# Query and key heads stored unrotated, forget gates in steps, and a second phase in written TensorE order

## The chip, the cores and the metric

The kernel runs on one core of one Trainium2 chip. The metric is the device time of one execution in microseconds. Before the change it is 2653.64 us, the median of 3 runs (2651.35 to 2655.81).

## The reference

The reference is a trunk of two layers over 1024 positions of width 1024, float32. Layer 0 mixes with gated DeltaNet heads and a short convolution (`mixer_ab`), layer 1 with HGRN2 heads and dilated sliding-window attention (`mixer_cd`). Each layer adds a SwiGLU feed-forward network of 2816 hidden columns, and a normalisation closes the trunk. The change lies in `mixer_cd`, cut here to what matters:

```python
hq, hf, hi, hg, sq, sk, sv = split_cols(h @ w_in, CD_SPLITS)      # 4 x 512 and 3 x 1536 columns
f_gate = lb + (1 - lb) * sigmoid(hf);  log_f = log(f_gate);  k_in = (1 - lb) * sigmoid(-hf)
o_c = hgrn2_recurrence(silu(hq), k_in, hi, log_f)                 # 4 heads, 128 x 128 state, chunks
o_c = rms_norm(o_c, norm_g) * sigmoid(hg)
sq, sk = rope(sq, pos), rope(sk, pos)                             # 3 patterns x 4 heads of 128
for p, (window, dilation) in enumerate(((128, 1), (512, 4), (2048, 16))):
    o_p, lse_p = dilated_window_attention(sq[p], sk[p], sv[p], window, dilation)
o_d = sum over p of softmax(lse)[p] * o_p
return concatenate([o_c, o_d]) @ w_out

def rope(x, pos):                                                 # x1, x2: halves of the 128 columns
    return concatenate([x1 * cos - x2 * sin, x1 * sin + x2 * cos])
```

## The kernel before

Activations stand transposed, features on the 128 partitions and positions along the free dimension, in two halves of 512 positions. Weights and activations are split into a high and a low float32r part, and each product of a 128x128 block runs as three matmuls (`mm3`, lines 126 to 128). `split` (lines 102 and 103) makes the two parts: a ScalarE cast for the high one and a VectorE subtraction for the low one.

**The pair loop.** The class `Up` (line 253) computes two column blocks of a projection at a time, as one product of 2x2 blocks: the halves of the positions by the halves of the inner dimension, with seven products instead of eight (`p1`, `p2`, `p5`, `p6`, `p7` and the two at the end of a pair). A product is 12 matmuls of 512 columns. GpSimd makes the sums of weight blocks (`sums`, `sums_late`, lines 302 to 308), `part_a` to `part_d` split them. In both feed-forward networks `Up.pair` runs in this way for 22 pairs. `Pairs` (line 726) is a subclass that does it for 16 pairs of layer 1's input projection: 12 pairs of a query and a key head (`"k"`, pattern, head), and 4 of an HGRN2 forget gate and query (`"f"`, head). Its loop starts at line 898. Everything in it, on TensorE, VectorE, ScalarE, GpSimd and the DMA queue of SyncE, stands in an order written out by hand (`manual_schedule`): an engine takes its instructions in the order of the source, and what stands behind a waiting one waits too.

A finished block c of a rotated head goes through `roped` (line 775): ScalarE copies the two halves of the partitions crosswise (L778, L779), GpSimd multiplies the copy by the sines (L780), VectorE multiplies c by the cosines (L781) and adds (L785, or L789 with a strided store which puts the positions of a dilated pattern in order of their residue classes). The result goes to DRAM (`qk`). `forget` (line 794) makes the gates of one block in four parts. These are generators; the loop advances them with `next` at chosen places. The copies and sums that TensorE waits for stand between them: `snap` (L338), the copy of x in `p6` (L365), the copy and sum in `add22` (L825, L826), `add11` (L342), and `row1`'s sum (L838).

Raw weights come through two buffers of a ring and a spare one; those for the next pair are asked for at the end of a pair and at the start of the next.

**The second phase.** `mixer_cd` (line 1659) projects the values with plain `mm3` products: `hgrn_v` for HGRN2 (two calls of eight row blocks), `swa_v` for a pattern of attention, `hgrn_gates` for the output gates. After each piece they call `tick(cost)`, which advances two generators in turn, `chain` (the units of HGRN2, a head and a half each) and `local` (the attention). A turn of `local` computes the scores of one quarter of an attention head, the transposes of the quarter before, and the outputs of the one before that; a head is four turns. `Attend` loads q and k of a head from DRAM, `combine` merges the three patterns. `rate` sets how many turns a unit of cost gives.

In this phase no order is written: a planner puts the instructions of each engine in order by the place in the source and by the time at which it expects them to be ready, and draws instructions forward whose inputs and buffers are there.

A unit of HGRN2 (line 1710) computes decays for seven block sizes on VectorE and ScalarE (`decayed`, L1722 to L1730), products of 32x32 blocks (`blocks`, L1738), the update of the state (L1819), outputs (L1823, L1826), their norm (L1829 to L1838) and a product with a diagonal (L1844), in seven pieces of TensorE work.

Of the kernel before, what the change touches and what calls it, by code (L numbers as in the profile page):

```python
# [54 lines left out]
def hybrid_trunk_kernel(ctx: ExitStack, tc: tile.TileContext, x_t, w_all, w_down, w_ba, vecs, c_f, c_i, c_rope, out):  # L55
# [670 lines left out]
    class Pairs(Up):  # L726

        early = True
        HEADS = (("k", 0, 0), ("k", 0, 1), ("k", 0, 2), ("k", 0, 3), ("k", 1, 0), ("f", 0), ("k", 1, 1), ("k", 1, 2),
                 ("f", 1), ("k", 1, 3), ("k", 2, 0), ("f", 2), ("k", 2, 1), ("k", 2, 2), ("f", 3), ("k", 2, 3))  # L730

        def __init__(self, left):
# [7 lines left out]
            self.snaps = self.right = None  # L740

        def src(self, kind, f):
# [20 lines left out]
        def turned(self):  # L763
            return self.right.tile([P, HT], F32, tag="r", name="r", bufs=2)

        def done(self, f, i, half, c, psum=False):

            kind = self.HEADS[f]
            if kind[0] == "k":
                return self.roped(self.qk[kind[1:]][i, :, half], kind[1], half, c, psum)  # L770
            if i == 0:
                return self.forget(self.bkq[kind[1], half], kind[1], c)
            return self.query(self.bkq[kind[1], half], c, psum)

        def roped(self, dst, p, half, c, psum):
            t = slice(half * HT, (half + 1) * HT)
            r = self.turned()
            S.copy(r[0:64], c[64:128])  # L778
            S.copy(r[64:128], c[0:64])  # L779
            G.tensor_tensor(r, r, self.rope[:, 1, t], op=MULT)  # L780
            V.tensor_tensor(c, c, self.rope[:, 0, t], op=MULT)  # L781
            yield
            if p == 0:
                d = r if psum else c
                V.tensor_tensor(d, c, r, op=ADD)  # L785
            else:
                n = (None, 4, 16)[p]
                d = self.scratch("d")
                V.tensor_tensor(d.rearrange("p (r i) -> p i r", r=n), c.rearrange("p (i r) -> p i r", r=n),  # L789
                                r.rearrange("p (i r) -> p i r", r=n), op=ADD)  # L790
            dma(dst, d)
            yield

        def forget(self, dst, h, c):
            r = self.turned()
            V.tensor_scalar(c, c, -44.0, None, op0=MAX)
            S.activation(r, c, AF.Exp, scale=-1.0)
            S.activation(c, r, AF.Identity, bias=onec[:, 0:1])
            yield
            V.reciprocal(c, c)  # L800
            d = self.scratch("d")
            G.tensor_tensor(d, r, c, op=MULT)
            yield
            S.activation(r, c, AF.Ln, scale=self.omlb[:, h:h + 1], bias=self.lb[:, h:h + 1])
            S.activation(d, d, AF.Copy, scale=self.omlb[:, h:h + 1])
            dma(dst[1], d)
            yield
            for j in range(4):
                t = slice(j * P, (j + 1) * P)
                V.tensor_tensor_scan(c[:, t], onec[:, 0:1].to_broadcast([P, P]), r[:, t], 0.0, op0=MULT, op1=ADD)  # L810
            dma(dst[0], c)
            yield

        def query(self, dst, c, psum):
            r = self.turned()
            S.activation(r, c, AF.Tanh, scale=0.5)
            yield
# [80 lines left out]
        def pair(self, f, count, b11, b21, b22, t1, t2, t3, t4):  # L898
# [31 lines left out]
            if more:  # L930
                s = self.sums(an, bn)
# [1445 lines left out]
```

## Time and profile before

| what | us |
|---|---|
| median of 3 runs | 2653.64 |
| the profiled execution | 2653.08 |
| its span, from the first to the last instruction | 2651.3 |
| pair loop of layer 1, pairs 3 to 14 | 285.6 (1216.4 to 1502.0) |
| last pair | 30.2 (1502.0 to 1532.2) |
| second phase, up to the output projection | 381.9 (1532.2 to 1914.1) |

Layer 0 and its feed-forward network lie ahead of these stretches, the output projection and the feed-forward network of layer 1 behind them. The page's busy time of TensorE is 97% of the span; since matmuls are pipelined and their ends are modelled, the number of matmuls in a stretch says more about it than the busy time.

### The profile page before, as it was taken

To read this page: it belongs to the slowest core of one execution; us is meant where nothing else is said; L and a number is where in the kernel's file an instruction comes from. 1 tells how busy PE (TensorE), PEld (TensorE's weight loads), DVE (VectorE), ACT (ScalarE), POOL (GpSimd) and SP (SyncE) were. 2 spreads that over 40 slices of the span, in tenths; PEclk is the share of its full clock that TensorE was granted. 3 is DMA by queue.
4 is the path that set the end of the run, shared out by engine and by line. 5 is a ranking of instruction groups with operands and counts; after the bars stand their busy time and mean duration, and the time that the engine had idled before them with its cause. 6 is when DMAs were issued, how large, how long until landed. Compare 5 with 4: busy or idle time off the path is not lost. (4 is left out here: it accounts for less than half of the span.)

```text
span 2651.3 us, 37844 instructions
## 1 busy us (share of the span) xinstructions
PE 2571.7 (97%) x14163; PEld 2131.2 (80%) x14163; DVE 1750.8 (66%) x2873; ACT 1076.2 (41%) x1779; POOL 656.1 (25%) x552
## 2 busy tenths in 40 slices
PE   8999999999999999998888899999999999999998
PEld 6888888888888888887666687978788888888887
DVE  7887775685655665578777776358867655556554
ACT  5432123343333344445545544445444333334442
POOL 1110111333333200135545411000023433331001
PEclk9999999999999999999999999999999999999999
DMA  4425447325566687623323344666672555658853
GB/s 140 139 94 167 110 144 237 117 95 179 175 210 204 223 288 265 195 80 111 100 96 104 111 160 128 168 157 199 178 237 71 168 171 184 216 200 290 279 176 119
DMA packets 273480, 443.12 MB, mean 167 GB/s; under 512 B 48624, under 2 KB 133136, under 8 KB 273040
## 3 DMA queue, kind: packets, MB, share of 16 engines
q1 hardware_dynamic: 273296, 440.71, 51.3%
q8 instruction: 111, 1.82, 0.3%
q14 instruction: 73, 0.60, 0.1%
HBM read 300.55 MB, written 140.07 MB: 166 GB/s over the span
## 5 line engine op out<-in xcount | busy, mean ns | idle before, releaser
L103 DVE TENSOR_TENSOR w<-raw,w 128x1024 fp32r<-128x1024 f32 (+1 forms) x323 | 387.4, 1204 | 142.3 <-ACT w L102 141.0
L102 ACT CAST w<-raw 128x1024 fp32r<-128x1024 f32 (+1 forms) x323 | 307.9, 958 | 284.8 <-PE psu L128 152.2
L126 PE MATMUL psu<-hnh,w 128*128 128x512 f32 x848 | 338.4, 399 | 7.6 <-ACT w L102 7.6
L127 PE MATMUL psu<-hnl,w 128*128 128x512 f32 x848 | 332.0, 392 | 0.1
L128 PE MATMUL psu<-hnh,w 128*128 128x512 f32 x848 | 332.0, 391 | 0.0
L126 PEld LDWEIGHTS psu<-hnh,w 128*128 128x128 f32 x848 | 160.2, 189 | 40.1 <-ACT w L102 7.6
L128 PEld LDWEIGHTS psu<-hnh,w 128*128 128x128 f32 x848 | 159.8, 188 | 34.6 <-DVE w L103 0.8
L127 PEld LDWEIGHTS psu<-hnl,w 128*128 128x128 f32 x848 | 160.3, 189 | 32.7 <-DVE hnl L2162 0.7
L187 POOL TENSOR_TENSOR acc<-acc,sq 128x512 f32<-128x512 f32 x48 | 70.5, 1469 | 430.2 <-ACT sq L183 410.7
L302 POOL TENSOR_TENSOR ws<-raw 128x512 f32<-128x512 f32 x54 | 75.7, 1403 | 399.0 <-DMA raw<-in_dram 255.4
L103 DVE TENSOR_TENSOR w<-ws,w 128x1024 fp32r<-128x1024 f32 x51 | 73.2, 1436 | 97.7 <-ACT w L102 97.7
L103 DVE TENSOR_TENSOR hidq<-hr,hidq 128x1024 fp32r<-128x1024 f32 x72 | 82.4, 1145 | 77.3 <-ACT hidq L102 77.1
L126 PE MATMUL psu<-t3h,w 128*128 128x512 f32 x240 | 98.7, 411 | 24.6 <-ACT u L365 24.4
L102 ACT CAST hidq<-hr 128x1024 fp32r<-128x1024 f32 x72 | 70.2, 979 | 103.7 <-DMA hr<-ts 62.3
L126 PE MATMUL psm<-hidq,w 128*128 128x512 f32 (+1 forms) x275 | 106.0, 385 | 0.0
L127 PE MATMUL psm<-hidq,w 128*128 128x512 f32 (+1 forms) x275 | 105.8, 385 | 0.0
L128 PE MATMUL psm<-hidq,w 128*128 128x512 f32 (+1 forms) x275 | 105.8, 385 | 0.0
L780 POOL TENSOR_TENSOR r<-r,rope 128x512 f32<-128x512 f32 x48 | 80.6, 1682 | 97.9 <-ACT r L779 90.9
L126 PE MATMUL psu<-t4h,w 128*128 128x512 f32 x240 | 95.0, 396 | 9.0 <-ACT c L825 8.5
L126 PE MATMUL psg<-b22h,w 128*128 128x512 f32 x216 | 85.8, 397 | 12.6 <-DVE c L826 12.6
L127 PE MATMUL psu<-t3l,w 128*128 128x512 f32 x240 | 96.7, 403 | 0.0
L128 PE MATMUL psu<-t3h,w 128*128 128x512 f32 x240 | 96.7, 403 | 0.0
(507 smaller groups left out, 6775.2 us busy)
## 6 DMA issues: line engine op xcount, KB each, us to landing
raw<-in_dram SPq DMA_DIRECT2D x227, 512.0 KB, 4.0
sd<-in_dram SPq DMA_DIRECT2D x44, 512.0 KB, 3.9
hid<-hid SPq DMA_DIRECT2D x88, 256.0 KB, 2.8
sd<-sd SPq DMA_DIRECT2D x44, 512.0 KB, 3.4
hr<-ts SPq DMA_DIRECT2D x40, 512.0 KB, 4.6
raw<-sd SPq DMA_DIRECT2D x40, 512.0 KB, 4.4
hd<-h SPq DMA_DIRECT2D x48, 256.0 KB, 3.8
h<-hd SPq DMA_DIRECT2D x48, 256.0 KB, 5.8
```

Of the source, the lines that this page charges most:

```text
L102: S.copy(hi, src)
L103: eng.tensor_tensor(lo, src, hi.bitcast(F32), op=SUB)
L126: T.matmul(o, lh, rh, start=first and i == 0, stop=False, **kw)
L127: T.matmul(o, lh, rl, start=False, stop=False, **kw)
L128: T.matmul(o, ll, rh, start=False, stop=last and i == n - 1, **kw)
L187: (eng or G).tensor_tensor(a, a, q, op=ADD)
L302: G.tensor_tensor(s[:, HT:], b[:, :HT], b[:, HT:], op=ADD)
L780: G.tensor_tensor(r, r, self.rope[:, 1, t], op=MULT)
```

## The change

A head's q and k are stored as they come out of the projection, in the order of the residue classes. The rotation moves to the second phase: `Attend` loads q and k, and loads each once more with the two halves of the partitions exchanged (`rs`, four DMAs), and GpSimd multiplies the exchanged copy by the sines (`sines`) and q or k by the cosines, and adds (`roped`): twelve operations of 128x512 a head. There are three tables of cosines and sines, one for each order of positions. The work of a head's rotation is spread over the turns of the head before.

The gates are computed for both halves together, in seven steps, of which a pair takes three (`step`). The order of the 16 pairs changes. Raw weights are asked for a pair earlier, for even pairs into the spare buffer and a new one, for odd pairs into the ring.

The second phase has TensorE in written order. A unit of HGRN2 has its block products in two runs, and outputs in a third; its norm is taken from sums that ScalarE makes beside the square, and it scales before four transposes, which take the place of the product with a diagonal. HGRN2's values go through DRAM. The second `hgrn_v` stands ahead of the second pattern. `combine` scales and adds with the weight as a scalar operand, 128 columns at a time.

```diff
-        HEADS = (("k", 0, 0), ("k", 0, 1), ("k", 0, 2), ("k", 0, 3), ("k", 1, 0), ("f", 0), ("k", 1, 1), ("k", 1, 2),
-                 ("f", 1), ("k", 1, 3), ("k", 2, 0), ("f", 2), ("k", 2, 1), ("k", 2, 2), ("f", 3), ("k", 2, 3))
+        HEADS = (("k", 0, 0), ("k", 0, 1), ("k", 0, 2), ("f", 0), ("k", 1, 0), ("k", 1, 1), ("f", 1), ("k", 1, 2),
+                 ("k", 1, 3), ("f", 2), ("k", 2, 0), ("k", 2, 1), ("f", 3), ("k", 2, 2), ("k", 2, 3), ("k", 0, 3))
...
+        def fetch(self, n):
+            if n >= len(self.HEADS):
+                return
+            if n % 2:
+                self.coming[n] = self.raw("g", n), self.raw("u", n)
+                return
+            t = self.right.tile([P, DM], F32, tag="raw", name="raw", bufs=1)
+            self.coming[n] = self.raw("g", n, True), t
+            dma(t, self.src("u", n))
...
-            r = self.turned()
-            S.copy(r[0:64], c[64:128])
-            S.copy(r[64:128], c[0:64])
-            G.tensor_tensor(r, r, self.rope[:, 1, t], op=MULT)
-            V.tensor_tensor(c, c, self.rope[:, 0, t], op=MULT)
...
+        def total(self, f, i, half, c, y):
+            if (self.HEADS[f][0], i) == ("f", 1):
+                V.tensor_tensor(c, c, y, op=ADD)
+                return self.query(f, half, c)
+            d = self.place(f, c)
+            o, a, b = self.streams(f, d, c, y)
+            V.tensor_tensor(o, a, b, op=ADD)
+            self.keep(f, i, half, d)
...
+        def forget(self, h):
+            cs = [self.kept_f.pop((h, half)) for half in range(NH)]
+            rs = [self.scratch("fr") for _ in cs]
+            for c, r in zip(cs, rs):
+                V.tensor_scalar(c, c, -44.0, None, op0=MAX)
+                S.activation(r, c, AF.Exp, scale=-1.0)
             yield
+            for c, r in zip(cs, rs):
+                S.activation(c, r, AF.Identity, bias=onec[:, 0:1])
             yield
+            for half, (c, r) in enumerate(zip(cs, rs)):
+                V.reciprocal(c, c)
+                d = self.fresh("kk")
+                V.scalar_tensor_tensor(d, r, self.omlb[:, h:h + 1], c, op0=MULT, op1=MULT)
+                dma(self.bkq[h, half][1], d)
+                yield
+            for c, r in zip(cs, rs):
+                S.activation(r, c, AF.Ln, scale=self.omlb[:, h:h + 1], bias=self.lb[:, h:h + 1])
             yield
...
+        def pair(self, f, b11, b21, b22, t1, t2, t3, t4):
             n = f + 1
             self.p1(f, b11)
+            if f == 3:
+                self.fetch(n)
             self.add22(f - 1)
...
+                self.part_d(f, self.a)
+                self.fetch(n + 1)
+            self.step()
             self.p2(f, b21, psm())
             g = self.snap(f)
...
             self.add11(f, g)
+            an, bn = self.coming.pop(n)
+            s = self.sums(an, bn)
+            self.row2(f - 1, t4)
+            self.part_a(n, an)
+            self.sums_late(an, bn, s)
+            self.row1(f - 1, b22)
+            self.step()
             self.p6(f, t2)
             self.p5(f, t1, psg())
+            self.part_b(n, s)
+            self.part_c(n, bn)
+            self.a = an
+            self.step()
+            self.p7(f, t3)
...
                 def __init__(self, h, p):
+                    if p not in table:
+                        table.clear()
+                        table[p] = tl("rope", (2, 2, HT))
+                        dma(table[p], c_rope[p].rearrange("p z (b t) -> p z b t", b=2))
+                    self.table, self.w = table[p], []
+                    for src in (pairs.qk[p, h][i] for i in range(2)):
+                        w = tl("rs", (2, HT), 2)
+                        dma(w[0:64], src[64:128])
+                        dma(w[64:128], src[0:64])
+                        self.w.append(w)
...
+                def sines(self, i):
+                    for b in range(2):
+                        G.tensor_tensor(self.w[i][:, b], self.w[i][:, b], self.table[:, 1, b], op=MULT)
+                def roped(self, i):
...
+                    for b in range(2):
+                        G.tensor_tensor(c[:, b], c[:, b], t[:, b], op=MULT)
+                        G.tensor_tensor(c[:, b], c[:, b], w[:, b], op=ADD)
...
+                for p in range(3):
+                    for j in range(4):
+                        d, x, w = t[0][:, j, 0:P], t[p][:, j, 0:P], w3[:, p, j:j + 1]
+                        if p:
+                            V.scalar_tensor_tensor(d, x, w, d, op0=MULT, op1=ADD)
+                        else:
+                            S.activation(d, x, AF.Copy, scale=w)
...
+                def begin():
+                    u = first.pop()
+                    second.append(u)
+                    u.load()
+                    todo[:] = [lambda: [u.sines(i) for i in (1, 0)], lambda: u.roped(1), lambda: u.roped(0), prepare]
...
+                    if not now and second:
+                        while todo:
+                            todo.pop(0)()
+                        now += [second.pop(), 0]
+                        if first:
+                            begin()
+                    elif todo:
+                        todo.pop(0)()
...
-            due, rate = [0.0, 0.0], [0.0, 4 / 3]
+            due, rate = [0.0, 0.0], [0.0, 1.0]
...
+            with tc.manual_schedule(engines={E.PE}):
+                hgrn_v(0, pairs.first, lambda cost: None, range(0, 4))
+                have_v[0] = 1
+                hgrn_v(0, pairs.first, tick, range(4, 8))
+                for p in (1, 2, 0):
+                    swa_v(p, tick)
+                    ready += [(h, p) for h in range(4)]
+                    rate[0] = 1.4 if p == 0 else 0.8
+                    if p == 1:
+                        hgrn_v(1, wload(("cd", 10), ("cd", 11)), tick)
+                        have_v[0] = 2
+                hgrn_gates(tick)
+                while ready or busy[0]:
+                    next(loc)
```

More of the change, by code (lines that the diff above doesn't have):

```diff
@@ L1798, in hgrn @@
[L1798 to L1808 removed]
+                last = half == NH - 1
@@ L1809, in hgrn @@
+                for r in range(4):
+                    z = slice(r * 32, (r + 1) * 32)
+                    S.copy(attn[z, :, z], ac[z])
                 before = [states.get(h)] + [st[:, c, :] for c in range(3)]
@@ L2111, in local @@
                     line = [line[1], nxt]
-                    busy[0] = any(line) or bool(late or now or ahead or ready)
+                    busy[0] = any(line) or bool(late or now or second or first or ready)
                     yield
@@ L2131, in mixer_cd @@
                 G.memset(diag[i], 0.0)
[L2132 to L2144 removed]
+            E = mybir.EngineType
+            with tc.manual_schedule(engines={E.PE}):
[12 more added lines that the diff above has]
+                    next(loc)
     es = ExitStack()
```

512 lines of the change are left out of this document (220 added, 292 removed).

## The prediction

> **What bounds the kernel now.** I read the page first. TensorE is busy 97% of the span, but the page says that a busy PE is not a PE at its peak, so the next view was the table of busy time by stretches, cut at the first matmuls of the stages. Its columns are: stretch, length, then busy us and count of PE, weight loads, DVE, ACT and POOL, granted clock, DMA share, GB/s.
>
> ```profile
> span 2651.3 us, 37844 instructions
> PE 2571.7 (97%) x14163; PEld 2131.2 (80%) x14163; DVE 1750.8 (66%) x2873; ACT 1076.2 (41%) x1779; POOL 656.1 (25%) x552
> ...
> 1138.90:1216.40 77.50, 73.39 (x322) 60.20 (x321) 71.20 (x76) 37.58 (x50) 31.76 (x18) 0.96 0.28 92
> 1216.40:1502.00 285.60, 246.34 (x1009) 194.70 (x1008) 210.32 (x209) 147.32 (x207) 152.49 (x94) 0.95 0.29 96
> 1502.00:1532.20 30.20, 25.65 (x109) 19.95 (x108) 24.26 (x26) 20.38 (x27) 12.09 (x8) 1.00 0.41 132
> 1532.20:1655.00 122.80, 119.48 (x1424) 100.42 (x1424) 80.54 (x202) 51.91 (x103) 16.16 (x24) 1.00 0.47 155
> 1655.00:1740.00 85.00, 85.00 (x642) 76.19 (x640) 32.01 (x118) 39.57 (x115) 3.44 (x6) 1.00 0.63 160
> 1740.00:1806.70 66.70, 64.24 (x809) 51.97 (x805) 47.05 (x170) 36.26 (x106) 6.70 (x12) 1.00 0.59 163
> 1806.70:1914.10 107.40, 100.84 (x985) 85.85 (x983) 92.00 (x328) 54.54 (x148) 6.67 (x11) 0.98 0.63 185
> 2100.00:2400.00 300.00, 300.00 (x1326) 248.39 (x1325) 179.13 (x237) 101.88 (x142) 105.56 (x80) 1.00 0.59 196
> ```
>
> The last row is the yardstick: the feed-forward loop of layer 1 issues 1326 matmuls in 300.0 us, 0.2262 us each, with no gap. The pair loop of the CD projection (second row of stretches) has the same products and issues 12 pairs x 84 = 1008 of them; at 0.2262 that is 228.0 us, and it takes 285.6. So 57.6 us of TensorE are lost there, and 30.2 - 108 x 0.2262 = 5.8 in the last pair. The reader is to see that this loop, and not the kernel as a whole, has a second limit. The view of waits for that loop names it:
>
> ```profile
> POOL r L780 <- ACT r L779: 71.3, 23, 8.0
> ACT r L778 <- DVE c L826: 36.6, 8, 6.0
> PE psu L126 <- ACT u L365: 24.4, 11, 4.9
> DVE d L789 <- POOL r L780: 20.5, 11, 4.6
> PE psg L126 <- DVE c L826: 12.6, 10, 2.9
> PE psu L126 <- ACT c L825: 6.7, 6, 1.5
> ```
>
> PE waits for plain copies out of PSUM (L365, L825) and the add behind one (L826): 43.7 us. They are late because the rotation, ACT L778/L779 to POOL L780 to DVE L789, stands in the same queues in written order. In the phase behind it, 1532.2 to 1914.1 (381.9 us), the waits of PE are few:
>
> ```profile
> PE psu L2067 <- DVE ol L2062: 4.8, 2, 3.2
> PE psg L1844 <- DVE e L1838: 2.4, 3, 1.0
> PE psg L1738 <- issue: 2.3, 2, 1.5
> PE psg L1793 <- DVE m L1730: 0.7, 1, 0.7
> ```
>
> **Part 1, the pair loop: about -60.** Out go, per rotated head, eight ACT half copies, four POOL products, four DVE products by the cosine and the adds; in come only the sums of the products (strided for two patterns).
>
> ```profile
> L103 DVE TENSOR_TENSOR w<-ws,w 128x1024 fp32r<-128x1024 f32 x13 | 22.5, 1734 | 0.0
> L789 DVE TENSOR_TENSOR d<-psu,r 128x512 f32<-128x512 f32 x7 | 7.6, 1088 | 0.0
> L342 DVE TENSOR_TENSOR gt<-gt,psm 128x512 f32<-128x512 f32 x13 | 8.8, 676 | 0.0
> L800 DVE RECIPROCAL gt<-gt 128x512 f32<-128x512 f32 x4 | 13.4, 3342 | 0.0
> L338 ACT COPY gt<-psu 128x512 f32<-128x512 f32 x13 | 7.6, 581 | 0.2
> L804 ACT ACT_TABLE_LOAD x8 | 10.3, 1283 | 0.1
> L780 POOL TENSOR_TENSOR r<-r,rope 128x512 f32<-128x512 f32 x43 | 73.6, 1714 | 74.0 <-ACT r L779 71.3 <-DVE w L103 2.5
> L308 POOL TENSOR_TENSOR raw<-raw,ws 128x512 f32<-128x512 f32 x13 | 23.5, 1811 | 0.0
> ```
>
> DVE then has, per rotated pair, three strided sums at 1.09, three weight remainders at up to 1.73 and half a one: about 9 us of the pair's 228.0/12 = 19.0. The feed-forward loop hides 179.1/300 = 60% of DVE, 11.3 us a pair, without a gap, so TensorE should set the pace; what is late next is the strided sums, which only stores and a free PSUM bank wait for. A forget gate adds, over the three pairs in which its seven steps run, two reciprocals (6.7), small work of about 5 and a few table loads at 1.28; its longest piece, 3.34, is shorter than the 5.4 us (24 matmuls) between a product's end and the next one that needs its copy. The gates cost 0 if those 5.4 us hold, and 8 x 3.34 = 26.7 if every reciprocal lands ahead of a wait; I take 4, near the first, since the feed-forward row shows none. The strided copy on ACT in row2 isn't in the trace: between 0.58 (L338) and the DVE ratio 1088/676 of it, 0.93; nothing waits for it but a DMA. Fetching raw weights a pair ahead issues the same DMAs earlier on SP's queue, behind stores that wait for DVE; with 19 us of lead I cost that at nothing, and at 4 us a pair if the lead is gone. Loop: 57.6 - 4 = -53.6. Last pair: 5.8 less the one copy and one add that still stand between p7 and the last two products (0.58 + 0.68, so 1.2): -4.6. The opening (first stretch: 322 x 0.2262 = 72.8 of 77.5) can give 0 to 4; I take 2. Sum: -60.2.
>
> **Part 2, the second phase: about +5.** Rows of that phase, then the queues of DVE and POOL at one place of the loop before:
>
> ```profile
> L1844 PE MATMUL psg<-e,e 128*128 128x128 f32 x64 | 8.9, 281 | 2.5 <-DVE e L1838 2.4
> L1800 PE MATMUL psg<-cf,kk 128*128 128x128 f32 x32 | 5.1, 280 | 0.0
> L1838 DVE TENSOR_TENSOR e<-cf,rr 128x512 f32<-128x512 f32 x8 | 5.5, 693 | 8.7 <-POOL rr L1836 8.7
> L1833 DVE TENSOR_REDUCE ss<-e 128x4 f32<-128x512 f32 x8 | 5.5, 685 | 3.4 <-ACT e L1831 3.3
> L1846 DVE TENSOR_SCALAR e<-psg,vec 128x512 f32<-128x512 f32 x8 | 6.0, 748 | 2.7 <-PE psg L1844 2.6
> k<-qk SPq DMA_DIRECT2D x12, 512.0 KB, 4.8
> ```
> ```profile
> 1359.97 2.32 DVE L103 TENSOR_TENSOR w<-ws,w 128x1024 fp32r<-128x1024 f32 x1
> ...
> 1365.13 1.23 DVE L103 TENSOR_TENSOR w<-raw,w 128x1024 fp32r<-128x1024 f32 x1 [1.13 <-ACT w L102]
> ...
> 1359.91 1.30 POOL L307 TENSOR_TENSOR raw<-raw 128x512 f32<-128x512 f32 x1
> 1361.17 2.28 POOL L308 TENSOR_TENSOR raw<-raw,ws 128x512 f32<-128x512 f32 x1
> ```
>
> HGRN2's last product becomes four transposes a half: 8.9 to 5.1, -3.8. Three longer runs, two turns apart, should remove the waits at L1844, L1793 and L1738: 3 to 5 of the rows above, I take 4. DVE loses the reduction, the diagonal and the scaling by the gain (5.5 + 5.5 + 6.0 = 17 us in all), which is off the path.
>
> Against that stand the rotations: 12 attention heads x 12 GpSimd products or sums of 128x512. One alone is 1.30 (L307). The queues show what it does to DVE: the remainder issued at 1359.97, under L307, took 2.32 for 1.23, that is, it began its work when L307 ended at 1361.21; and L308, issued at 1361.17, took 2.28, waiting out that remainder. So a POOL operation and a DVE operation with two SBUF operands exclude each other. Per POOL operation DVE loses between 0 and 2.32 - 1.23 = 1.1; the phase-long means lie between (w<-ws 1.73 in the loop against 1.23 free: 0.5), and I take 0.55: 144 x 0.55 = 79 us. DVE has 381.9 - (80.5 + 32.0 + 47.1 + 92.0) = 130 idle, so on the whole it fits, but not in the last stretch, where 15.4 are idle and three heads (36 operations, 20 us) fall: about 5 over. A rotation takes 12 x 1.30 = 15.6 free, 12 x 1.71 = 20.6 at the mean of L780, 27.4 if each is blocked as L308 was; the last stretch gives 22.4 attention turns (16 ticks at 1.4) in 107.4 us, 4.8 a turn, 19.2 a head. At 20.6 the scores, which in written order hold all of TensorE behind them, come 1.4 late per head, 5 in four heads. I take 10 for both. The written order leaves 54.4 turns inside the projections where 55 are needed (three turns stay empty while the second pattern's values aren't there): the last combination stands bare, +3. The partner halves, three sine tables and the value round trip add some 20 MB to a DMA share of 0.47 to 0.63; I cost it at nothing, because q and k are asked for early, and at 4.8 (the k row) per load if not. SP issues some 75 DMAs more at 0.33 (L1922, quoted below), 25 us of a queue that is mostly empty; but a partner load that waits for its tile to be released by POOL holds the weights and stores behind it on SP, and this is where a late rotation would spread. Phase: -3.8 - 4 + 10 + 3 = +5, ends -12 and +35.
>
> The Trainium skill, "SBUF — State Buffer", section "Who interferes with whom", says that VectorE and GpSimd share one port pair as an exclusive lock, and that whichever starts second is fully blocked; the two rows above agree. By it the sum stays as it is, but it speaks against this change: rival A is its full price.
>
> **Sum.** The profiled execution took 2653.1 us (span 2651.3 and 1.8 around it), the median of the runs is 2653.6: no difference to speak of. 2653.1 - 60.2 + 5 = 2598.
>
> **Rivals.** A, the shared port decides the second phase: each POOL operation holds DVE 0.95 instead of 0.55 (137 us). DVE's own work is 251.6 - 17 - 5 = 230; its busiest stretch reached 92.0/107.4 = 0.857, and (230 + 137)/0.857 = 428 is 46 more than 381.9. Then 2653.1 - 60.2 + 46 = 2639. For it: the rows of L103 and L308, and that decays come in rows of short two-operand operations. Against: POOL is idle in the first stretch and can work ahead there. It decides from 0.68 us an operation on.
>
> B, slower than before: no head start. The first head of each pattern is loaded, rotated and scored in one turn of the written order. If its loads and products aren't drawn forward, TensorE stands for table and operands (4.8) and 12 x 1.71: 25.3, three times, 76: 2653.1 - 60.2 - 7.8 + 76 = 2661. It decides from 68/3 = 22.7 us a start on. Against it: before, the first q load was issued at 1545.6 and its scores began at 1625.9, 80 us later, so loads are drawn forward.
>
> ```profile
> L1950 PE MATMUL psm<-k,q x128: 270/379/631, 1625.9 to 1893.1; 128*128 128x256 f32 x88, 128*128 128x128 f32 x40
> L1922 SPq DMA_DIRECT2D q<-qk x8: 319/330/1066, 1545.6 to 1846.4; - x8
> ```
>
> C, the pair loop keeps half of its loss, because the forget steps put reciprocals and table loads ahead of the copies: +27 (the bound above), 2625. D, the second phase gains too (-18: all waits of the four rows, the transposes, and rotations wholly under idle DVE): 2575.
>
> **Numbers.** Forecast 0.60 (2598, own range 2580 to 2618), A 0.14, B 0.04, C 0.11, D 0.11. The range 2568 to 2638 holds the forecast, C, D and the nearer half of A. A measurement here tells 0.2% (5.3 us) from no change; faster holds in all cases but B and the upper tail of A: 0.94; same 0.02; slower 0.04.
>
> **What would show it.** Right: the twelve pairs take 229 to 238 us with 1008 matmuls; no wait of PE for L365's copy; POOL busy some 200 to 250 us in the second phase, two-operand DVE groups there with means above their present ones, PE's waits gathered in the last stretch at the scores. Wrong: pairs still above 21 us (part 1), or a second phase over 400 us (A), or three PE waits over 20 us at the first scores of a pattern (B).

## The result, and the profile after

The changed kernel takes 2675.64 us, the median of 4 runs (2671.94 to 2678.84), against 2652.49 us (2650.50 to 2655.81) of the kernel before in the same comparison: a ratio of 1.0089 with a 95% interval of 1.0076 to 1.0101. It is slower by 23 us, where 2598 us and "faster" were forecast. The profiled execution took 2674.45 us, 21.4 us more than the 2653.08 us of before.

The table of busy time by stretches of the kernel after, cut at the same stages as before; columns as in the prediction. The last stretch but one runs from the end of the pairs to the first matmul of the feed-forward network's norm, so it holds the second phase and the output projection:

```profile
1138.90:1212.10 73.20, 70.34 (x322) 57.83 (x322) 63.69 (x70) 33.46 (x44) 25.91 (x14) 1.00 0.31 109
1212.10:1440.55 228.45, 228.45 (x1010) 189.22 (x1008) 144.47 (x142) 99.68 (x133) 75.29 (x50) 1.00 0.32 115
1440.55:1466.00 25.45, 25.45 (x115) 21.05 (x114) 13.39 (x20) 11.26 (x15) 1.03 (x3) 1.00 0.62 212
1466.00:1989.10 523.10, 444.57 (x4048) 376.83 (x4048) 344.15 (x838) 230.70 (x631) 214.34 (x158) 0.92 0.63 185
2120.00:2420.00 300.00, 300.00 (x1325) 248.43 (x1324) 177.81 (x238) 101.62 (x142) 104.15 (x80) 1.00 0.58 195
```

The same view of the kernel before, for the stretch from the end of its pairs to the same norm:

```profile
1532.20:1967.80 435.60, 423.26 (x4085) 358.71 (x4085) 281.71 (x849) 204.38 (x501) 41.88 (x59) 1.00 0.61 181
```

The pair loop did what was forecast: 12 pairs in 228.45 us instead of 285.6, with 1.00 of the clock and no idle time, the yardstick's pace. With the opening (73.20 for 77.50) and the last pair (25.45 for 30.20) it gives 66.2 us. All of that and 21.3 more is lost behind it: 523.10 for 435.60 is +87.5. TensorE stands idle there for 523.10 - 444.57 = 78.5 us instead of 12.3, and its busy time grew by 21.3 with no more matmuls. The granted clock fell from 1.00 to 0.92. The clock record of this stretch knows full and half clock only; 14 pieces of it, of 3.4 to 10.2 us and 85 us together, are at half clock.

The waits of TensorE in that stretch, after (engine, tile and line, what ended the wait: us in all, times, longest):

```profile
PE psg L1834 <- ACT e L1758: 20.2, 7, 5.5
PE psu L2088 <- DVE ol L2081: 20.0, 10, 6.3
PE psm L1968 <- DVE stat L1974: 13.9, 3, 5.5
PE psm L2026 <- DVE pt L2017: 6.6, 2, 4.5
```

Transposes (L1834), the combination (L2088), scores (L1968) and outputs (L2026) all wait a little, for VectorE or for ScalarE's copy L1758; for a rotated operand of GpSimd they wait 0.3 us in all. What happens to VectorE shows in its own groups. Line, engine, operation, names and shapes, count, then busy us and mean ns, after:

```profile
L1719 DVE TENSOR_TENSOR m<-m,q 128x256 f32<-128x256 f32 x56 | 39.7, 709 | 1.6 <-DMA q<-bkq 1.5
L1711 DVE TENSOR_TENSOR m<-b 128x256 f32<-128x256 f32 x56 | 37.6, 676 | 26.7 <-PE psg L1727 23.9 <-DMA kk<-bkq 2.7
L1715 DVE TENSOR_TENSOR m<-m,kk 128x256 f32<-128x256 f32 x48 | 34.7, 724 | 1.9 <-ACT m L1714 1.7
L1713 DVE TENSOR_TENSOR m<-b 128x256 f32<-128x256 f32 x48 | 30.6, 638 | 0.0
L1974 DVE CUSTOM_DVE_ANT_0 sc<-psm,cf 128x256 f32<-128x256 f32 x44 | 17.7, 419 | 7.0 <-PE psm L1968 7.0
```

The same four groups of the decays in the kernel before:

```profile
L1730 DVE TENSOR_TENSOR m<-m,q 128x256 f32<-128x256 f32 x56 | 23.7, 423 | 1.5 <-ACT m L1728 1.5
L1722 DVE TENSOR_TENSOR m<-b 128x256 f32<-128x256 f32 x56 | 23.6, 427 | 14.6 <-PE psg L1738 14.0 <-PE psg L1793 0.3
L1726 DVE TENSOR_TENSOR m<-m,kk 128x256 f32<-128x256 f32 x48 | 20.3, 424 | 6.0 <-ACT m L1725 5.6
L1724 DVE TENSOR_TENSOR m<-b 128x256 f32<-128x256 f32 x48 | 20.4, 425 | 0.0
```

In this kernel the tiles `psm`, `psg` and `psu`, which TensorE writes, lie in PSUM, and VectorE's other operands in SBUF. The four groups, each with two operands in SBUF, take 638 to 724 ns in the mean, where they took 423 to 427. The group of L1974 has one operand in PSUM and takes the same 419 ns (416 before).

Two places of the timeline after, with start, us, engine, line and count, show how this reaches TensorE (a row that is three operations in one says x3 and the time from its first to its last):

```profile
1840.06 1.19 DVE L2071 TENSOR_TENSOR tmp<-w,cm 128x4 f32<-128x4 f32 x1
1841.28 1.18 DVE L2073 TENSOR_TENSOR dn<-dn,tmp 128x4 f32<-128x4 f32 x1
...
1857.24 0.17 DVE L2071 TENSOR_TENSOR tmp<-w,cm 128x4 f32<-128x4 f32 x1
1857.44 0.16 DVE L2073 TENSOR_TENSOR dn<-dn,tmp 128x4 f32<-128x4 f32 x1
1857.64 0.18 DVE L2074 RECIPROCAL tmp<-dn 128x4 f32<-128x4 f32 x1
1857.85 2.23 DVE L2076 TENSOR_TENSOR w<-w,tmp 128x4 f32<-128x4 f32 x3
1860.00 3.75 DVE L2081 SCALAR_TENSOR_TENSOR ol<-cm,w,ol 128x128 f32<-128x128 f32 x6
...
1841.18 2.48 POOL L1944 TENSOR_TENSOR q<-q,rope 128x512 f32<-128x512 f32 x2
1857.57 4.98 POOL L1937 TENSOR_TENSOR rs<-rs,rope 128x512 f32<-128x512 f32 x4 [11.46 <-DMA rs<-qk]
...
1856.44 1.06 PE L2026 MATMUL psm<-vp,pt 128*128 128x128 f32 x8
1863.01 0.48 PE L2088 MATMUL psu<-cf,ol 128*128 128x128 f32 x1 [5.51 <-DVE ol L2081]
...
1865.88 0.63 PE L126 MATMUL psu<-hnh,w 128*128 128x512 f32 x1
1866.31 0.63 PE L127 MATMUL psu<-hnl,w 128*128 128x512 f32 x1
```

`combine` divides four numbers a row by their sum. While GpSimd is idle, one such step takes 0.16 us (L2073 at 1857.44). Beside GpSimd's products it takes 1.18 (1841.28): an operation on 4 columns costs as much as one of GpSimd's on 512. At 1857.57 GpSimd starts four products of a head's rotation, three steps take 2.23 us and the sums behind them 3.75 for six. TensorE waits 5.51 us for the end of that chain. In the kernel without rotations (below) such a step takes 157 ns and such a sum 347 in the mean; by these, an estimate, 3.4 of the 5.51 us come from GpSimd. Then TensorE's matmuls of 512 columns start 0.43 us apart (1865.88, 1866.31), where 0.2262 is its pace at full clock, and the stretch around it was granted half the clock:

```profile
1862.00:1868.50 6.50, 5.18 (x14) 3.86 (x15) 2.44 (x8) 0.59 (x1) 0.55 (x1) 0.50 0.61 149
```

The clock fell inside the wait, some 4.4 us after the last matmul and before the next one:

```profile
1860.00:1861.00 1.00, 0.00 (x0) 0.00 (x0) 1.00 (x2) 0.69 (x2) 1.00 (x2) 1.00 0.00 0
1862.00:1863.00 1.00, 0.00 (x0) 0.00 (x0) 1.00 (x3) 0.00 (x0) 0.55 (x1) 0.50 0.00 0
```

The same is to be found all over the stretch: TensorE has 12 waits of 2.9 us or more in it, and at each of them, within 4 us of its end, a piece at half clock begins. In the kernel before, the one wait of that size in its stretch (3.2 us) has such a piece too.

The Trainium skill, "TensorE: Matmul & The Clock Gate", section "Part 1: The HAM clock gate", says that the array falls to half its clock after an idle window of about 3.4 us; the trace agrees, with the wait of 5.51 us and these rows. Two of the 12 waits, of 2.95 and 3.05 us, are shorter than that window and have a piece at half clock all the same.

### The profile page after: what moved, and what is told of

Read it like the earlier page. It is cut to its first block, busy times and chain, and to the rows that moved or that the text cites. A ratio compares the mean times of both kernels' runs of the same rounds, so it can differ in the third digit from the quotient of the medians.

```text
span 2672.6 us, 37762 instructions
## 1 busy us (share of the span) xinstructions
PE 2572.3 (96%) x14131; PEld 2143.1 (80%) x14131; DVE 1727.8 (65%) x2786; ACT 1041.8 (39%) x1815; POOL 733.3 (27%) x600
## 5 line engine op out<-in xcount | busy, mean ns | idle before, releaser
L302 POOL TENSOR_TENSOR ws<-raw 128x512 f32<-128x512 f32 x54 | 81.8, 1514 | 428.5 <-DMA raw<-in_dram 299.6
L103 DVE TENSOR_TENSOR w<-ws,w 128x1024 fp32r<-128x1024 f32 x51 | 66.6, 1306 | 113.8 <-ACT w L102 113.8
L308 POOL TENSOR_TENSOR raw<-raw,ws 128x512 f32<-128x512 f32 x51 | 67.0, 1314 | 161.1 <-DVE w L103 161.1
L393 POOL TENSOR_TENSOR hid<-hid,c 128x512 f32<-128x512 f32 x44 | 62.3, 1416 | 126.0 <-ACT hid L392 125.8
L126 PE MATMUL psu<-t4h,w 128*128 128x512 f32 x240 | 93.7, 391 | 0.5 <-ACT c L372 0.5
L127 PE MATMUL psu<-t4l,w 128*128 128x512 f32 x240 | 93.4, 389 | 0.0
L128 PE MATMUL psu<-t4h,w 128*128 128x512 f32 x240 | 93.4, 389 | 0.0
L126 PE MATMUL psu<-t3h,w 128*128 128x512 f32 x240 | 93.4, 389 | 0.0
```

Source lines behind the costliest of these rows:

```text
L103: eng.tensor_tensor(lo, src, hi.bitcast(F32), op=SUB)
L126: T.matmul(o, lh, rh, start=first and i == 0, stop=False, **kw)
L127: T.matmul(o, lh, rl, start=False, stop=False, **kw)
L128: T.matmul(o, ll, rh, start=False, stop=last and i == n - 1, **kw)
L302: G.tensor_tensor(s[:, HT:], b[:, :HT], b[:, HT:], op=ADD)
L308: G.tensor_tensor(a[:, HT:], a[:, HT:], s[:, :HT], op=SUB)
```

## The experiments

Each kernel below is the changed one with the edit shown. The theory from the trace: a GpSimd product or sum of two SBUF operands keeps VectorE's two-operand operations waiting, these stand in chains that TensorE waits for, and the written TensorE order lets it do nothing else meanwhile.

### The rotation, and the written order

Without the rotation (`sines` and `roped` return at once; q and k are used unrotated, and all loads stay):

```diff
 def sines(self, i):
+    return
 def roped(self, i):
+    return
```

> The changed kernel without the twelve GpSimd operations of a head: q and k are used unrotated, so the attention is that of unrotated heads; all loads stay. Theory 2: VectorE's busy time in the second phase falls from 315 to about 235 us, the phase to about 390 and the kernel to 2580 to 2600. Theory 1: the phase falls by less than 30 us and the kernel stays above 2645. Theory 3: the waits at L1834 stay at 20 us.

Measured: 2597.86 us (2594.49 to 2602.05), ratio 0.9796 (0.9781 to 0.9810). The 144 operations cost 2675.64 - 2597.86 = 78 us, not 10, as the second theory had it. Its stretch from the end of the pairs to the norm, and its group for L1719:

```profile
1466.00:1908.80 442.80, 419.48 (x4049) 359.46 (x4048) 250.53 (x838) 228.36 (x631) 17.13 (x14) 0.98 0.74 218
```
```profile
L1719 DVE TENSOR_TENSOR m<-m,q 128x256 f32<-128x256 f32 x56 | 23.5, 419 | 1.8 <-DMA q<-bkq 1.7
```

VectorE does the same 838 operations in 250.53 instead of 344.15 us: 93.6 us, or 0.65 for each of the 144 operations on GpSimd.

The second phase in the planner's order:

```diff
-with tc.manual_schedule(engines={E.PE}):
+with ExitStack():
```

> The changed kernel with its second phase in the planner's TensorE order again; all else as changed. Theory 1 (the written order costs it: TensorE stands at the head of its line where other products were ready): the second phase falls from 470 us by 60 or more, the kernel to 2590 to 2615. Theory 2 (GpSimd's rotations hold VectorE through the shared port, and the order only shows it): VectorE's busy time in the phase stays near 315 us and the kernel stays above 2645. Theory 3 (a third PSUM bank in one turn, 20 us of waits at L1834): about 2655.

Measured: 2655.94 us (2653.38 to 2662.96), ratio 1.0020 (1.0010 to 1.0029). 20 us of the loss hang on the order in which TensorE takes its work. The first theory, by which the order made the whole loss, is out.

Both edits together:

> Both at once: no rotation (unrotated q and k are used) and the planner's TensorE order. It gives the floor of the phase: 355 to 370 us, the kernel 2555 to 2575. If theories 1 and 2 are two sides of one thing (late VectorE work that only a written order makes TensorE stand for), it is no more than 15 us under the better of the two single runs; if they are two costs that add, it is lower than each by what the other gave.

Measured: 2584.57 us (2578.88 to 2590.24), ratio 0.9745 (0.9728 to 0.9762), above the floor of 2555 to 2575 that was expected. Without rotations the written order costs 13 us, fewer than the 20 beside GpSimd. The waits show where most of it lies; first without rotations in written order, then in the planner's:

```profile
PE psg L1834 <- ACT e L1758: 12.9, 7, 2.5
```
```profile
PE psg L1834 <- ACT e L1758: 3.5, 5, 1.5
```

L1834 are the transposes that close the HGRN2 unit before. One of these waits in the timeline of the changed kernel:

```profile
1529.34 1.30 ACT L1714 ACTIVATE m<-m 128x512 f32<-128x512 f32 x2 [1.90 <-DVE m L1713]
1530.55 0.57 ACT L1758 COPY e<-psg 128x512 f32<-128x512 f32 x1
...
1531.17 1.11 PE L1834 MATMUL psg<-cf,e 128*128 128x128 f32 x4 [2.95 <-ACT e L1758]
```

They start when ScalarE's copy L1758 has emptied a PSUM buffer, which stands in ScalarE's queue behind exponentials that wait for VectorE's decays. In written order TensorE stands at them until then.

Those transposes one turn later:

```diff
-                ending[1]()
                 ms = [decayed(8, *bkq), decayed(16, *bkq)]
                 yield
+                ending[1]()
```

> The changed kernel with the four transposes that close a unit of HGRN2 one turn later, so that they don't ask for a third bank of a tag that has two in the turn that fills both. Theory 3: the waits of TensorE at L1834 (20.2 us in seven places) go, and the kernel falls by 15 to 25 us, to about 2655. Theories 1 and 2: they move to the next place where VectorE or ScalarE is late, and the kernel moves by less than 8 us.

Measured: 2667.78 us, ratio 1.0064 (1.0047 to 1.0081): 8 us less; the main loss stays. But the 8 us don't come from where the third theory looked for them: TensorE's waits at L1834 stay at 17.0 us in seven places, after 20.2, and those of the scores (L1968) fall from 13.9 to 6.4. So the theory of the third bank is out.

### What of the rotation costs

Three things could cost: rotated operands that come late, a long queue on GpSimd (the power of HGRN2's norm, L1825, stands in it), or the port through which GpSimd and VectorE both read SBUF, the prediction's shared port. The first kernel runs twelve such operations a head on the exchanged copies and tables alone, whose results nobody reads (q and k are used unrotated):

```diff
-    c, w, t = self.c[i], self.w[i], self.table[:, 0]
-    if len(c.shape) == 4:
-        w, t = (x.rearrange("p b (s i) -> p b s i", s=16) for x in (w, t))
+    c, w, t = self.w[i], self.w[i], self.table[:, 0]
...
-        G.tensor_tensor(c[:, b], c[:, b], w[:, b], op=ADD)
+        G.tensor_tensor(c[:, b], c[:, b], t[:, b], op=ADD)
```

> The changed kernel with the same twelve GpSimd operations a head, at the same places, but all of them on the exchanged copies and the tables: q and k are used unrotated, and no score waits for GpSimd. What it tells apart: the rotated operands come late (then it falls to where no rotation stood, 2590 to 2615), or the operations cost by running beside VectorE, whoever needs their results (then VectorE's busy time in the second phase stays near 315 us and the kernel at 2660 to 2680). I expect the second.

Measured: 2692.45 us (2684.49 to 2695.89), ratio 1.0145 (1.0125 to 1.0165). No score waits for a rotation here, and it is slower still. But it isn't a clean test: VectorE waits 63.9 us for the power in it, and 20.4 in the changed kernel, since all twelve operations of a head stand in the queue at once. So it was run again with the power left out (`V.tensor_scalar(rr, ss, 1.0, None, op0=ADD)` in its place):

> The twelve operations of the decoy, whose results nobody reads, and the power left out as well (the heads aren't normalised, q and k not rotated), so that no engine waits for a result of GpSimd. Theory (the read port alone makes the cost): 2650 to 2685, at least 50 us above the 2598 us without operations on GpSimd. Rival (the decoy's cost came from the power standing behind the twelve operations in GpSimd's queue): 2598 to 2625.

Measured: 2672.54 us (2671.59 to 2675.61), ratio 1.0076 (1.0060 to 1.0093). No engine waits for a result of GpSimd in the second phase here, and the kernel is 75 us above the one without rotations. VectorE's two-operand groups are as slow as in the change, but TensorE's waits lie in other places, most of them at the transposes that close an HGRN2 unit (L1833 here):

```profile
L1719 DVE TENSOR_TENSOR m<-m,q 128x256 f32<-128x256 f32 x56 | 40.6, 725 | 1.6 <-ACT m L1714 1.5
```
```profile
PE psg L1833 <- ACT e L1758: 61.5, 7, 15.4
```

So GpSimd's reads alone can cost this much; that 75 is so near to 78, with 61.5 us of waits where the change has 20.2, is in part chance. The power alone, left out of the changed kernel:

> The changed kernel with the power of HGRN2's norm left out (a VectorE sum of four columns in its place), so that VectorE's scaling (L1829) never waits for GpSimd; the heads aren't normalised. The waits of VectorE for L1825 were 20.4 us in eight places. If they stand on the path, the kernel falls by 12 to 25 us, to 2650 to 2663; if they lie beside other waits, by less than 6.

Measured: 2673.46 us, ratio 1.0077 (1.0062 to 1.0092): 2 us, within the spread of the runs.

The other way round, GpSimd busy and its queue full, but without reading SBUF: 16 memsets of 128x1024 a head in place of the rotation, which is left out.

```diff
-    for b in range(2):
-        G.tensor_tensor(self.w[i][:, b], self.w[i][:, b], self.table[:, 1, b], op=MULT)
+    for b in range(3):
+        G.memset(self.w[i], 0.0)
...
-    for b in range(2):
-        G.tensor_tensor(c[:, b], c[:, b], t[:, b], op=MULT)
-        G.tensor_tensor(c[:, b], c[:, b], w[:, b], op=ADD)
+    for b in range(5):
+        G.memset(self.w[i], 0.0)
```

> The changed kernel with sixteen GpSimd memsets of 128x1024 a head in place of the twelve operations (0.96 us each by the one before, 15.3 us a head against 15.6): GpSimd's queue is as long, but it reads no SBUF; q and k are used unrotated. If the cost is the shared port, VectorE's busy time falls to about 230 us and the kernel to 2595 to 2625, what is left being the power of the norm (L1825), which still stands behind the memsets. If the cost is the length of GpSimd's queue, the kernel stays above 2650.

Measured: 2598.06 us (2597.45 to 2600.89), ratio 0.9797 (0.9783 to 0.9812), the same as without any rotation. The stretch of this kernel, and two of its groups:

```profile
1466.00:1912.20 446.20, 419.99 (x4052) 359.72 (x4050) 260.57 (x838) 227.92 (x631) 196.03 (x206) 0.98 0.73 217
```
```profile
L1719 DVE TENSOR_TENSOR m<-m,q 128x256 f32<-128x256 f32 x56 | 23.9, 427 | 1.6 <-DMA q<-bkq 1.5
L1941 POOL MEMSET rs<- 128x1024 f32 x120 | 113.6, 955 | 4.3
```

GpSimd is busy for 196 us in it, 214 in the changed kernel; yet L1719 takes 427 ns and not 709. So GpSimd's time doesn't make the 78 us; its reads do. VectorE isn't quite alone, though. It is busy for 260.57 us where it was for 250.53 without any work of GpSimd, above all in small copies within SBUF, such as this one, which took 172 ns there:

```profile
L2036 DVE COPY ol<-stat 128x8 f32<-128x8 f32 x8 | 5.5, 692 | 2.0 <-ACT sc L1971 1.9
```

This cost the kernel nothing that the runs can tell. The Trainium skill, "SBUF — State Buffer", section "Who interferes with whom", has it so: a VectorE instruction with two SBUF inputs contends with a GpSimd instruction that reads SBUF, and not with one that only writes. The two kernels agree: 2672.54 us with the reads and 2598.06 with writes alone.

### How much of it VectorE's idle time covers

The prediction let VectorE's loss "fit" into its idle time. So the twelve operations were shared out between the two engines: all on VectorE, or only the sums and products with the cosines, or only the products with the sines.

```diff
-G.tensor_tensor(self.w[i][:, b], self.w[i][:, b], self.table[:, 1, b], op=MULT)
+V.tensor_tensor(self.w[i][:, b], self.w[i][:, b], self.table[:, 1, b], op=MULT)
...
-G.tensor_tensor(c[:, b], c[:, b], t[:, b], op=MULT)
-G.tensor_tensor(c[:, b], c[:, b], w[:, b], op=ADD)
+V.tensor_tensor(c[:, b], c[:, b], t[:, b], op=MULT)
+V.tensor_tensor(c[:, b], c[:, b], w[:, b], op=ADD)
```

> The changed kernel with the twelve operations of a head on VectorE. They are 144 x 0.60 = 86 us of VectorE, as much as it lost to GpSimd (315 - 227 = 88), so its busy time stays near 315 us. If VectorE's total is what counts, the kernel stays at 2660 to 2680. If it is the long single holds and the power behind the rotations, it falls to 2600 to 2640.

> The other way round: only the 48 products with the sines on GpSimd, cosines and sums on VectorE. Theory (proportional): 2631, give or take 10. Rival (the idle time swallows them): 2605 to 2615.

> The products with the sines on VectorE, the products with the cosines and the sums on GpSimd: 96 operations on GpSimd instead of 144 (none: 2609 us, 144: 2676 us). Theory (each operation costs its share wherever it stands): 2653, that is 2609 + 96/144 of 67 us, give or take 10. Rival (VectorE's idle time swallows the first of them and only the excess counts, as the prediction's sum had it): 2612 to 2630.

| operations on GpSimd | on VectorE | us | ratio to before (95%) |
|---|---|---|---|
| 144 (the change) | 0 | 2675.64 | 1.0089 (1.0076 to 1.0101) |
| 96 (`sines_on_vector`) | 48 | 2668.51 | 1.0063 (1.0046 to 1.0080) |
| 48 (`sums_on_vector`) | 96 | 2628.37 | 0.9908 (0.9892 to 0.9925) |
| 0 (`vector_rotation`) | 144 | 2609.07 | 0.9835 (0.9821 to 0.9850) |

The stretch behind the pairs in the last three of these, in the order of the table:

```profile
1466.00:1983.90 517.90, 441.07 (x4062) 375.29 (x4061) 340.51 (x889) 232.15 (x633) 152.53 (x113) 0.92 0.63 187
```
```profile
1466.00:1944.70 478.70, 433.35 (x4050) 366.73 (x4049) 337.12 (x935) 230.38 (x632) 85.85 (x62) 0.95 0.68 203
```
```profile
1466.00:1925.40 459.40, 427.76 (x4058) 363.20 (x4057) 334.31 (x985) 230.77 (x632) 19.76 (x17) 0.97 0.71 211
```

With all of it on VectorE the kernel falls to 2609 us, so VectorE's total, by which it would have stayed at 2660 to 2680, isn't what counts. VectorE is busy for 334.31, 337.12, 340.51 and, in the change, 344.15 us. It gains nothing from handing the rotation over: what GpSimd's reads take from it (93.6 us) is more than the same 144 operations cost on VectorE itself (334.31 - 250.53 = 83.8). And the time grows by 19 us for the first 48 operations, by 59 for 96, by 67 for 144. A share of 67 each would be 22 and 45; idle time that swallows the first would have given about 0 and 3 to 21, and that is refuted. That 96 cost nearly as much as 144 isn't explained by the share either, and stays open; the two steps also differ in which operations GpSimd keeps, the products with the sines or the others.

With as much busy time on VectorE, TensorE loses 64 us more when GpSimd rotates. Its idle time in these rows is 459.40 - 427.76 = 31.6 us with everything on VectorE and 78.5 in the change. That VectorE's own rotations stand where it has nothing else to do, while GpSimd's start when their data come and then block whatever VectorE has, fits this but was only argued.

### Shorter operations on GpSimd

The twelve operations cut into 48 of 128 columns:

```diff
-G.tensor_tensor(self.w[i][:, b], self.w[i][:, b], self.table[:, 1, b], op=MULT)
+for k in range(0, 512, P):
+    G.tensor_tensor(self.w[i][:, b, k:k + P], self.w[i][:, b, k:k + P], self.table[:, 1, b, k:k + P], op=MULT)
...
```

> Rotations on GpSimd as in the change, but each operation of 512 columns in four of 128 (48 instead of 12 a head). Theory (VectorE stands still for as long as GpSimd holds the read port, so the amount of data decides and not the length of one operation): no gain; 2670 to 2710, the upper part because each short operation brings a fixed time of its own. Rival (it is the length of a single exclusion that makes TensorE miss its operand; short ones are slept through): 2610 to 2650.

> Operations of 128 columns on GpSimd as in split, and the power behind the norm of HGRN2 left out (the heads aren't normalised), so that VectorE waits for nothing of GpSimd there. In split VectorE lost 60 us beside GpSimd's operations instead of 94, and waited 53 us for the power instead of 20. Theory (the shorter operations are cheaper at the port, and the late power hid it): 2640 to 2662. Rival (the power's lateness is covered, and short operations cost TensorE as much as long ones): 2680 to 2695.

Measured: 2691.21 us, ratio 1.0148 (1.0134 to 1.0162), and without the power 2692.98 us, ratio 1.0149 (1.0130 to 1.0168). The first came out within what its theory gave, and its rival fell. But VectorE waited 53.2 us for the power in it, and lost less beside GpSimd than before, which left room for a gain under the late power. The second run shows none: without the power it is as slow, VectorE is busy for 335 us again (310 in the first), and the theory that short operations are cheaper at the port fell. What the short operations did instead stands in the timeline of the second, VectorE and then GpSimd:

```profile
1518.72 16.45 DVE L1711 TENSOR_TENSOR m<-b 128x256 f32<-128x256 f32 x1 [5.30 <-PE psg L1727]
...
1517.47 6.64 POOL L1937 TENSOR_TENSOR rs<-rs,rope 128x128 f32<-128x128 f32 x16
1524.08 3.31 POOL L1949 TENSOR_TENSOR k<-k,rs 128x128 f32<-128x128 f32 x8
```

One VectorE operation of 0.42 us took 16.45 us, while GpSimd ran about 40 short ones back to back, of which the rows show the first ones. So VectorE didn't get the port each time that an operation of GpSimd ended.

### A version that beats both

With the rotation on VectorE, the two edits on the order were made again, one by one and together.

> Rotations on VectorE and the second phase in the planner's order. Theory (the written TensorE order turns every late VectorE result into TensorE time, 13 us of it without any rotation and 20 us with the rotations on GpSimd): 13 to 20 us below the 2609 us of the rotations on VectorE in written order, so 2589 to 2596. Rival (with the rotations on VectorE the written order costs nothing more, since the waits there are short): 2606 to 2612.

> Rotations on VectorE in written order, and the second of the closing parts of an HGRN2 unit one turn later. Theory (the 8 us that this gave beside GpSimd's rotations were waits for a VectorE that GpSimd held up): little is left of them, 2603 to 2609. Rival (the closing part stands too early whatever VectorE's speed): 8 us again, 2599 to 2603.

> All three: rotations on VectorE, closing part a turn later, planner's order. Theory (the planner draws work forward past a late operand by itself, so the place of the closing part no longer counts): the same as without the later place within 3 us, 2586 to 2599. Rival (both add up): 2578 to 2586.

Measured: 2597.83 us (2596.53 to 2598.42) in the planner's order, 2604.04 (2602.52 to 2605.62) with the later transposes, 2595.47 (2592.96 to 2596.50) with both, ratios 0.9793, 0.9817 and 0.9781 (0.9768 to 0.9795). The order costs 11 us here too, just below the 13 to 20 of the theory; the later transposes give 5 in written order, within what the theory gave, and 2 in the planner's order, as expected; both lie within the overlap of the intervals. The last is faster than the kernel before by 2.2% and leaves nothing of the computation out. Its stretch behind the pairs:

```profile
1466.00:1911.70 445.70, 423.96 (x4054) 358.94 (x4052) 333.92 (x983) 230.96 (x633) 18.80 (x14) 0.97 0.73 219
```

## Why the prediction was wrong

**Part 1 was right, a little low.** Forecast -60.2, measured -66.2. The loop gave 57.2 (228.45 us) against 53.6: the 4 us kept for the gates' reciprocals weren't needed. The last pair gave 4.75 against 4.6. The opening gave 4.3 against 2, a little over its upper bound of 4. TensorE has no wait at all in the twelve pairs, for L365's copy or anything else, so rival C is out.

**Part 2 failed: +87.5 against +5, and the term is the 10 us for the rotations.** They cost 78. The step had three sentences. "A POOL operation and a DVE operation with two SBUF operands exclude each other" held. "I take 0.55 ... 79 us" was near: 0.65 and 93.6 us. "DVE has 130 idle, so on the whole it fits" is the sentence that failed. VectorE is busy for 344.15/523.10 = 66% of the stretch after and was for 281.71/435.60 = 65% before; with the rotation on VectorE itself it is busy for 334.31/459.40 = 73%, and the kernel is 67 us faster. So its load isn't what decides. Its losses fall on operations that stand one behind the other in a chain which TensorE waits for, and idle time elsewhere gives nothing back. The timeline at 1841 and 1857 shows it on operations of 0.16 us, which no sum of busy times would have looked at; the series with 0, 48, 96 and 144 operations shows that the first 48 already cost.

**Two things made it dearer.** The written order: 20 us beside GpSimd, 13 without the rotations and 11 with VectorE's (forecast: 3, for a bare last combination). It was costed by counting turns, and not by asking which operand is late where TensorE has to stand and wait; without rotations that was above all ScalarE's copy ahead of L1834. And half the clock at each longer wait: 21.3 us of the 87.5 are longer busy time of TensorE and not idle time. The prediction had no term for it.

**The rest of part 2** (-7.8 for the transposes and the three runs): without rotations and in the planner's order the median is 66.6 us below before, against the 66.2 of the pairs, so hardly anything is left over by the medians. The profiled execution of that kernel, the lowest of its runs, shows 7.5 us less behind the pairs:

```profile
1466.00:1894.10 428.10, 414.50 (x4055) 354.18 (x4054) 249.65 (x839) 229.80 (x632) 17.36 (x14) 1.00 0.77 227
```

Between 0 and 7.5, then; the runs don't tell it closer.

**The rivals.** A, the port, was the right mechanism and got 0.14. Its price was wrong in the same way as the forecast's: it let VectorE's share of busy time decide, from 0.68 us an operation on, and gave +46. Measured were 0.65 us, below that point, and +87.5. Its sign, a second phase over 400 us, came: 470.0 (1466 to 1936). B didn't come: no wait of TensorE is over 6.3 us, and the first scores of a pattern wait for nothing of that kind. It had the sign right by accident. D is out; its 18 us also count 4 us of waits twice, since the waits of the four rows (10.2) and the transposes (3.8) make 14. Of the signs to look for, the busy time of GpSimd (205.51 us within 1466 to 1936) and the longer two-operand groups came as written; TensorE's waits didn't gather in the last stretch at the scores, but lie over all of it.

## What to carry to other kernels

In this kernel, products and sums of two SBUF operands on GpSimd took 0.65 us from VectorE each; VectorE did them itself in 0.68 (L1937 with everything on VectorE), or 0.58 by the growth of its busy time, so handing them over gained nothing. Memsets on GpSimd, which read nothing, cost the kernel nothing. VectorE's group with one operand in PSUM (L1974) kept its time; its small copies within SBUF did not, beside either kind. Price such a loss at the chain it delays, from the shortest operations in it, and not against the idle time of the engine. The written order of TensorE turned late operands into stalls, for 11 to 20 us, and stalls of some microseconds brought slow matmuls behind them.

The row for the 0.68, of the kernel with the rotation on VectorE:

```profile
L1937 DVE TENSOR_TENSOR rs<-rs,rope 128x512 f32<-128x512 f32 x48 | 31.3, 684 | 16.1 <-DMA rs<-qk 15.6 <-DMA rope<-in_dram 0.4
```

## What was not expected of the hardware

- A VectorE operation on 128x4 takes 0.16 us alone and 1.18 when GpSimd is running a product of 128x512: here the price of a collision was the length of GpSimd's operation (1.24 us) and not of VectorE's.
- Short GpSimd operations in a row can hold VectorE off for many of them: 16.45 us for one operation of 0.42, and cutting GpSimd's work into quarters made the kernel 16 us slower, not faster. The Trainium skill, "SBUF — State Buffer", section "Who interferes with whom", says that whichever issues first has the shared pair for its whole instruction and the other blocks. A wait over some 40 instructions isn't told by that.
- Nearly as many microseconds of memsets on GpSimd leave VectorE's two-operand groups as if alone (427 ns for L1719, 419 with GpSimd idle), while small copies within SBUF slow down beside them (692 ns for L2036, 172 with GpSimd idle).
- TensorE's clock: 0.92 of full in the stretch behind the pairs, 1.00 before the change, and 0.97 to 1.00 in the kernels without any of GpSimd's rotations. That the waits bring the half clock on is read from the rows at 1860 to 1863, where it fell with no matmul running, and from the 12 waits; no run held the clock fixed, so what of the 87.5 us it makes isn't measured by itself. The nearest figure is the 21.3 us of longer busy time.
